# Decoder trunk on one core: the latent projection as one pass over x, and the last output block cut in two

## The chip, the cores and the metric

The kernel runs on one core of a Trainium2 chip. The metric is device time in microseconds of one launch: the median of three runs of the kernel before is 759.71 us (758.45 to 760.53). One further execution was recorded by the profiler; every duration below comes from that one.

## What is computed

A trunk of two pre-norm residual layers on x of 256 tokens by 2048 features, in float32. Layer a is multi-head latent attention, layer b is MoBA attention, which at 256 tokens is causal attention with ALiBi. Cut to what the change touches:

```python
h    = rms_norm(x, norm_a)
proj = h @ w_in_a                         # 2048 x (512 + 256 + 64 + 2048)
q_lat, kv_lat, k_rope, gate = split(proj, [512, 768, 832])
q    = rms_norm(q_lat,  q_lat_norm)  @ w_q_up
kv   = rms_norm(kv_lat, kv_lat_norm) @ w_kv_up
x    = x + (attention(q, kv, k_rope) * silu(gate)) @ w_out_a
x    = x + moba_layer(x)                  # ends with  ... @ w_out_b, 2048 x 2048
```

The first 832 columns of `w_in_a` are "the latents" (`LAT`). The row scale of the RMS norm of x is applied after the projection; the gain is folded into x before it.

## The kernel before

x lies transposed in SBUF as 16 chunks k of 128 features by 256 tokens (tile `xt`). A float32 product is made of three fp32r products: x and the weights are each split into a high part (`xh`, `wh`) and a low part (`xl`, `wl`), and xh·wh + xh·wl + xl·wh are summed in PSUM. ACT makes the high part and DVE the low part, of x in `split_x` (L313, L314), of a weight chunk in `W.high` and `W.low` (L146, L150). A weight chunk is at most 1024 columns of 128 partitions, fetched by one DMA on SP's queue (L132); there are 4 buffers for raw chunks, 4 for high parts, 3 for low parts, and `run` fetches 4 chunks ahead of the step that TensorE is at.

Two builders make the steps of a product, one step for each k. `blk_rows` lets the weights move through TensorE past a stationary piece of x: tokens come out on partitions, in two token halves, each in one PSUM bank (`acc`, five banks). `blk_cols` does the reverse. All matmuls have the helper's line L198 and are chained, so TensorE runs them in exactly the order of the program.

That order comes from two lists. `main` holds the projections in the order in which they are written; `side` holds what lies between them (norms, transposes, scores, softmax, products with v) with the time after which each is assumed ready. `ordered` walks both with assumed costs and puts a side step in as soon as it is ready by that clock. `flip` transposes through a DMA on SP's queue.

The start: the latents were made in two passes over x, `lat0` for columns 0 to 415 and `lat1` for columns 416 to 831, 16 steps of 6 matmuls of 416 columns each. `lat0` has chunks of one k, one k, and then two k (832 columns); x arrives in pieces of one or two chunks of 128 features, each loaded just ahead of the weight chunk that needs it and split just ahead of the step. The four sums of squares (`squares`) lie in `lat1`, then come `gates[0]` (16 steps) and `gates[1][:HALF]` (3 steps) before the first head group, `group_a(0)`. The side chain of the latents runs meanwhile: `col_a` (sums over partitions, tile `ps_st`; the row scale `r_a`), `row_a` (`ps_r`), `lat_out` (scales the latents out of PSUM into `sf`, then their own norm), `lat_t` (transposes, `ps_lt`, and the split into `xt`), and then `group_a(0)` may start.

The end: `outs_b` are four blocks of 512 output columns, two PSUM banks each. `out_done_b` adds each bank to x (L856) and stores it as 256 KB on SP's queue (L857).

Of the kernel before, what the change touches and what calls it, by code (L numbers as in the profile page):

```python
# [26 lines left out]
ALU = mybir.AluOpType  # L27

P = 128
S = 256  # L30
DM = 2048
NC = DM // P
# [1 line left out]
EPS = 1e-6  # L34
WARM = 34
ACC = 5
HALF = 3


NR, NH, NW = 4, 4, 3  # L40
# [6 lines left out]
PA, PB, LO, TU, TUB, S1, S2A, S2B, S3 = 9000, 6000, 5000, 3000, 10000, 4800, 6000, 9000, 3000  # L47
# [6 lines left out]
LAT = QR + KVR + ROPE  # L54
# [22 lines left out]
def paired(v):  # L77

    return v.rearrange("p (g l e) -> p g e l", l=2, e=16)


def lines(v):

    return v.rearrange("p (g l e) -> p g l e", l=2, e=16)


def unpaired(v):

    return v.rearrange("p (g e l) -> p g l e", l=2, e=16)
# [3 lines left out]
def trunk(ctx: ExitStack, tc, xT, gains, cst, w_in_a, w_q_up, w_kv_up, w_out_a, w_in_b, w_out_b, outT):  # L93
    nc = tc.nc
# [7 lines left out]
    def acc(name):  # L102
        return pacc.tile([P, 512], F32, tag="acc", name=name)
# [86 lines left out]
    def chain(ins):  # L190

        if pe:
            tc.add_manual_dep(ins.ins, pe[-1].name, mybir.DependencyInfo(
                mybir.DependencyClass.NoSync, mybir.DependencyReason.DATA), reason="order")
        pe.append(ins.ins)

    def matmul(*args, **kw):
        chain(nc.tensor.matmul(*args, skip_group_check=True, **kw))  # L198
# [4 lines left out]
    def blk_rows(w, x, done, lag=PB, first=()):  # L203

        nk, n = w.shape[0] // P, w.shape[1]
        a = []

        def go(wt, c, k):
            xh, xl = x()
            if k == 0:  # L210
                a.extend(acc("acc") for _ in range(2))
            for t in range(2):
                ts = slice(t * P, (t + 1) * P)
                o = a[t][:, :n]
                matmul(o, xh[:, k, ts], paired(wt.h[:, c]), start=k == 0, stop=False)
                matmul(o, xh[:, k, ts], paired(wt.l[:, c]), start=False, stop=False)
                matmul(o, xl[:, k, ts], paired(wt.h[:, c]), start=False, stop=k == nk - 1)
            if k == nk - 1:
                done([a[t][:, :n] for t in range(2)])

        return _steps(w, go, 6 * (n / 2.4 + 2.5), lag, first, True)

    def blk_cols(w, x, done, lag=3000):

        nk, ns = w.shape[0] // P, w.shape[1] // P
        a = []

        def go(wt, c, k):
            xh, xl = x()
            if k == 0:  # L230
                a.extend(acc("acc") for _ in range(ns // 2))
            for s in range(ns):
                o = a[s // 2][:, (s % 2) * S:(s % 2 + 1) * S]
                ws = slice(s * P, (s + 1) * P)
                first = k == 0 and s % 2 == 0
                last = k == nk - 1
                matmul(o, wt.h[:, c, ws], paired(xh[:, k]), start=first, stop=False)
                matmul(o, wt.h[:, c, ws], paired(xl[:, k]), start=False, stop=False)
                matmul(o, wt.l[:, c, ws], paired(xh[:, k]), start=False, stop=last)
            if k == nk - 1:  # L240
                done(a)

        return _steps(w, go, 3 * ns * 109, lag)

    def _steps(w, go, cost, lag, first=(), moving=False):
        out, nc_w = [], 1024 // w.shape[1]
        nk = w.shape[0] // P
        k1 = 0
        for n in list(first) + [nc_w] * nk:
            k0, k1 = k1, min(k1 + n, nk)  # L250
            if k0 == nk:
                break
            wt = W(w[k0 * P:k1 * P], moving)
            for k in range(k0, k1):
                out.append(Step(lambda wt=wt, c=k - k0, k=k: go(wt, c, k), cost, lag if k == nk - 1 else 0,
                                w=wt if k == k0 else None))
        return out
# [30 lines left out]
    xh = one.tile([P, NC, S], F32R, name="xh")  # L288
    xl = one.tile([P, NC, S], F32R, name="xl")
# [21 lines left out]
    def split_x(c, gcol):  # L311
        xt = res["x"]
        res["split"] = nc.scalar.activation(xh[:, c], xt[:, c], AF.Copy, scale=col(gcol + c))  # L313
        nc.vector.scalar_tensor_tensor(xl[:, c], xt[:, c], col(gcol + c), xh[:, c].bitcast(F32),  # L314
                                       op0=ALU.mult, op1=ALU.subtract)
# [45 lines left out]
    def gate_done(g, rows):  # L361
        def done(a):
            for b in range(len(a)):
                ub = wk.tile([P, 2, S], F32, tag="gate", name="gate", bufs=4)
                gate_of[g + b] = ub
                x = wk.tile([P, 2, S], F32, tag="gx", name="gx")
                nc.vector.tensor_tensor(x, a[b].rearrange("p (h t) -> p h t", h=2),
                                        rows().unsqueeze(1).to_broadcast([P, 2, S]), op=ALU.mult)
                nc.scalar.activation(ub, x, AF.Tanh, scale=0.5)
                nc.vector.scalar_tensor_tensor(ub, ub, 1.0, x, op0=ALU.add, op1=ALU.mult)  # L370
        return done
# [90 lines left out]
    main, side = [], []  # L462
# [14 lines left out]
    def x_load(c0, c1):  # L477
        return lambda: nc.sync.dma_start(res["x"][:, c0:c1], xT[c0 * P:c1 * P].rearrange("(c p) t -> p c t", p=P))

    def x_split(c0, c1):  # L480
        def f():
            for c in range(c0, c1):
                split_x(c, G_NA)
        return Step(f, 0, 1000)

    def rest():
        with tc.issue_after(lat1[0].w.dma):
            nc.sync.dma_start(g_sb[:, G_QN:G_END], gains[:, G_QN:])
            nc.sync.dma_start(c_sb, cst[:, :C_COS])

# [31 lines left out]
    lat_acc = []  # L522

    def lat_out(i):
        def f():
            o = i * LAT // 2
            for t in range(2):
                nc.scalar.activation(lat[t][:, o:o + LAT // 2], lat_acc[i][t], AF.Copy, scale=scale_a["r"][:, t:t + 1])
            if i:
                lat_norm()  # L530
        return f

    lat_st = {}

    def lat_norm():
        st = one.tile([P, 2, 3], F32, name="lat_st")
# [50 lines left out]

    x_a = lambda: (xh, xl)
    rows_a = lambda: scale_a["rows"]
    lat0 = blk_rows(w_in_a[:, 0:LAT // 2], x_a, lat_acc.append, 0, (1, 1))  # L590
    lat1 = blk_rows(w_in_a[:, LAT // 2:LAT], x_a, lat_acc.append, 0)
    gates = [blk_cols(w_in_a[:, LAT + 256 * g:LAT + 256 * (g + 1)], x_a, gate_done(g, rows_a)) for g in range(8)]

    def v_tiles():
# [94 lines left out]
        return proj  # L689

    pieces = [(0, 1), (1, 2), (2, 4), (4, 6), (6, 8), (8, 10), (10, 12), (12, 14), (14, 16)]
    for i, (c0, c1) in enumerate(pieces):
        main += [x_split(c0, c1)] + lat0[c0:c1]
        for j in ((1, 2) if i == 0 else (i + 2,)):
            if j < len(pieces):
                lat0[pieces[j][0]].w.before = x_load(*pieces[j])
    squares = [Step(lambda j=j: sum_squares(ssq_a, 2 * j) or sum_squares(ssq_a, 2 * j + 1), 0, 2500) for j in range(4)]
    main += lat1[:2] + [Step(rest)]
    for j in range(4):
        main += [squares[j]] + lat1[2 * j + 2:2 * j + 4]  # L700
    main += lat1[10:] + gates[0] + gates[1][:HALF]
    col_a, row_a = token_scale(ssq_a, "a", scale_a, squares, tables)
    lo = [Step(lat_out(i), 0, LO, [col_a], b[-1:]) for i, b in enumerate((lat0, lat1))]
    lo[1].after.append(lo[0])
    lats = [Step(lat_t(b), 440, 2500, lo, bank=True) for b in range(3)]
    kr = Step(kr_t, 440, 2500, lats, bank=True)
# [26 lines left out]
    og = lambda: (ogh, ogl)  # L733
    outs_a = [blk_cols(w_out_a[:, 256 * j:256 * (j + 1)], og, out_done_a(j), 4000) for j in range(8)]

    for g in range(8):
        main += group_a(g)
        if g == 0:
            kr.after.append(main[-1])
        if g < 7:  # L740
            main += gates[g + 1][HALF:] + (gates[g + 2][:HALF] if g < 6 else [])
        gates[g][-1].after.append(row_a)
        if g > 3:
            gates[g][-1].after += [h[2] for h in heads[2 * g - 8:2 * g - 6]]
# [101 lines left out]
        side.extend(s for h in hb[-4:] for s in h)  # L846
        return gate + q + k + v

    def out_done_b(j):
        def f(a):  # L850
            xt = res["x"]
            for b in range(2):
                c = 4 * j + 2 * b
                y = xt[:, c:c + 2]
                both = lines(y.rearrange("p a b -> p (a b)"))
                nc.vector.tensor_tensor(both, unpaired(a[b]), both, op=ALU.add)  # L856
                nc.sync.dma_start(outT[c * P:(c + 2) * P].rearrange("(c p) t -> p c t", p=P), y)  # L857
        return f

    outs_b = [blk_cols(w_out_b[:, 512 * j:512 * (j + 1)], og, out_done_b(j)) for j in range(4)]  # L860

    col_b, row_b = token_scale(ssq_b, "b", scale_b, [outs_a[7][-1]], scales_b)
    side += [col_b, row_b]
# [3 lines left out]
    for b in outs_b:  # L867
        for i, s in enumerate(b):
            s.needs.append(hb[i][2])
    main += outs_b[0][:12] + outs_b[1][:6] + outs_b[0][12:] + outs_b[1][6:] + outs_b[2] + outs_b[3]  # L870
    run(ordered(main, side))


# [59 lines left out]
```

## Time and profile before

| | |
|---|---|
| median of three runs | 759.71 us (758.45 to 760.53) |
| the profiled execution | 760.14 us |
| its span, first to last instruction | 758.0 us |
| TensorE (PE) busy in the span | 746.2 us |
| VectorE (DVE) busy | 576.2 us |
| ScalarE (ACT) busy | 488.3 us |
| mean granted TensorE clock | 0.998 of full speed |

The profiled execution took 760.14 us, of which the span of its instructions is 758.0 us; 2.14 us lie around it. PE is TensorE's matmuls, DVE is VectorE, ACT is ScalarE, SP the engine whose queue issues nearly all DMAs. A row of the timeline gives the start in us from the start of the span, the duration, the engine, the line, the operation with its output and inputs by the program's names, and in brackets how long the engine had been idle and what released it. Matmuls are pipelined, so that one shows a longer duration than its distance to the next.

### The profile page before, as it was taken

How to read it: one execution, taken by the hardware profiler on the slowest of the kernel's cores; microseconds unless marked ns; L12 is line 12 of the kernel's file. 1: busy time of each engine (PE TensorE's matmuls, PEld its weight loads, DVE VectorE, ACT ScalarE, POOL GpSimd, SP SyncE). 2: the span in 40 equal slices, each digit the busy share in tenths (PEclk: the TensorE clock that was granted, in tenths of full speed). 3: DMA queues.
4: the chain of work that ended last, by engine and by line, in shares of the span. 5: the costliest groups of instructions: out<-in, count | busy, mean ns of one | idle time of the engine just before them, and what ended most of it. 6: DMA issues, size and time to landing. Idle time of an engine off the chain costs nothing.

```text
span 758.0 us, 14123 instructions
## 1 busy us (share of the span) xinstructions
PE 746.2 (98%) x5246; PEld 708.0 (93%) x5246; DVE 576.2 (76%) x1207; ACT 488.3 (64%) x1025; POOL 0.2 (0%) x4
## 2 busy tenths in 40 slices
PE   8999999999999899999999999999999999999997
PEld 7999999999999899998889988998889988899997
DVE  6888899898997585765888767886688857887552
ACT  7767888888877464545667566665567666574431
POOL 0000000000000000000000000000000000000000
PEclk9999999999999999999999999999999999999999
DMA  9866665666557966667886778876788778867771
GB/s 304 257 177 180 185 177 167 181 156 185 162 167 222 248 195 199 196 189 202 228 234 174 200 221 229 229 188 208 188 240 230 188 211 220 231 181 215 250 223 44
DMA packets 137973, 153.19 MB, mean 202 GB/s; under 512 B 47280, under 2 KB 94768, under 8 KB 137904
## 3 DMA queue, kind: packets, MB, share of 16 engines
q1 hardware_dynamic: 137760, 152.27, 70.7%
q8 instruction: 41, 0.67, 0.4%
q14 instruction: 28, 0.23, 0.1%
q10 hardware_dynamic: 144, 0.02, 0.0%
HBM read 139.68 MB, written 2.10 MB: 187 GB/s over the span
## 4 chain that ended last, share of the span: by engine, by line
PE 66%; DMA 1%; ACT 0%; DVE 0%; issue 0%; SPq 0%
PE acc L198 63%; PE ps_o L198 1%; PE ps_s L198 1%; DMA sm<-pz 1%; ACT wh L146 0%; DVE xt L856 0%; DVE pz L409 0%; PE ps_r L198 0%; PE ps_st L198 0%; ACT alibi L819 0%; SPq L408 0%; DVE pl L440 0%; ACT pz L407 0%; ACT ogh L455 0%; ACT sm L426 0%
## 5 line engine op out<-in xcount | busy, mean ns | idle before, releaser
L146 ACT ACTIVATE wh<-wr 128x1024 fp32r<-128x1024 f32 (+3 forms) x265 | 288.0, 1091 | 161.3 <-PE acc L198 144.0
L150 DVE TENSOR_TENSOR wl<-wr,wh 128x1024 fp32r<-128x1024 f32 (+3 forms) x265 | 313.9, 1187 | 90.6 <-PE acc L198 59.1
L198 PE MATMUL acc<-wh,xh 128*128 128x512 f32 (+1 forms) x448 | 168.6, 376 | 1.4 <-ACT wh L146 1.4
L198 PE MATMUL acc<-wl,xh 128*128 128x512 f32 (+1 forms) x448 | 167.5, 374 | 1.0 <-DVE wl L150 1.0
L198 PE MATMUL acc<-wh,xl 128*128 128x512 f32 (+1 forms) x448 | 167.2, 373 | 0.0
L198 PE MATMUL acc<-ogh,wh 128*128 128x256 f32 x512 | 142.7, 279 | 0.0
L198 PE MATMUL acc<-xh,wh 128*128 128x256 f32 x512 | 142.4, 278 | 0.0
L198 PE MATMUL acc<-ogl,wh 128*128 128x256 f32 x512 | 141.7, 277 | 0.0
L198 PE MATMUL acc<-ogh,wl 128*128 128x256 f32 x512 | 141.6, 276 | 0.0
L198 PE MATMUL acc<-xh,wl 128*128 128x256 f32 x512 | 140.8, 275 | 0.0
L198 PE MATMUL acc<-xl,wh 128*128 128x256 f32 x512 | 140.8, 275 | 0.0
L198 PEld LDWEIGHTS acc<-ogh,wl 128*128 128x128 f32 x512 | 99.1, 194 | 0.0
L198 PEld LDWEIGHTS acc<-ogl,wh 128*128 128x128 f32 x512 | 99.0, 193 | 0.1
L198 PEld LDWEIGHTS acc<-ogh,wh 128*128 128x128 f32 x512 | 99.0, 193 | 0.0
L198 PEld LDWEIGHTS acc<-xl,wh 128*128 128x128 f32 x512 | 98.2, 192 | 0.3
L198 PEld LDWEIGHTS acc<-xh,wh 128*128 128x128 f32 x512 | 98.2, 192 | 0.3
L198 PEld LDWEIGHTS acc<-xh,wl 128*128 128x128 f32 x512 | 98.3, 192 | 0.0
L198 PEld LDWEIGHTS acc<-wh,xh 128*128 128x128 f32 x448 | 84.7, 189 | 12.1 <-ACT wh L146 2.0
L198 PEld LDWEIGHTS acc<-wl,xh 128*128 128x128 f32 x448 | 84.7, 189 | 11.7 <-DVE wl L150 1.7
L198 PEld LDWEIGHTS acc<-wh,xl 128*128 128x128 f32 x448 | 84.7, 189 | 10.3
L198 PE MATMUL acc<-wh,xt 128*128 128x384 f32 (+1 forms) x192 | 57.5, 357 | 0.0
L409 DVE COPY pz<-sm 128x768 uint16<-128x768 uint16 x32 | 19.4, 605 | 22.7 <-DMA sm<-pz 22.4
(154 smaller groups left out, 841.1 us busy)
## 6 DMA issues: line engine op xcount, KB each, us to landing
wr<-w_in_b SPq DMA_DIRECT2D x128, 512.0 KB, 4.3
wr<-w_in_a SPq DMA_DIRECT2D x32, 512.0 KB, 4.0
wr<-w_out_a SPq DMA_DIRECT2D x32, 512.0 KB, 4.0
wr<-w_out_b SPq DMA_DIRECT2D x32, 512.0 KB, 4.6
wr<-w_in_a SPq DMA_DIRECT2D x15, 416.0 KB, 5.3
wr<-w_q_up SPq DMA_DIRECT2D x16, 384.0 KB, 3.8
wr<-w_kv_up SPq DMA_DIRECT2D x8, 512.0 KB, 3.8
xt<-xT SPq DMA_DIRECT2D x4, 512.0 KB, 5.7
```

The costliest lines, as they stand in the source:

```text
L146: nc.scalar.activation(self.ordering(self.h)[1], self.ordering(self.raw)[0], AF.Copy)
L150: nc.vector.tensor_tensor(self.ordering(self.l)[1], self.ordering(self.raw)[0], self.ordering(self.h.bitcast(F32))[1], op=ALU.subtract)
L198: chain(nc.tensor.matmul(*args, skip_group_check=True, **kw))
L409: nc.vector.tensor_copy(words(b), planes(a))
```

## The change

It does four things.

1. `blk_latents` replaces `lat0` and `lat1`: one pass over x, each k with both halves of the latents. The first k has two chunks of 416 columns, the other 15 have one chunk of 832 columns. The four accumulators (two halves, two token halves) are open at once. In a step the order is xh·wh, xl·wh, xh·wl, each for both token halves, first for the first half of the columns and then for the second.
2. x's pieces and the sums of squares follow that pass: a piece of two chunks is split, then come two steps of 12 matmuls; each `squares` step lies behind the piece that completes its four chunks. The load of the constants (`rest`) moves behind k = 5.
3. `HALVES` replaces `HALF`: 8 steps of `gates[1]` instead of 3 lie ahead of `group_a(0)`, then 6, 4 and from there on 3 as before.
4. The last 512 output columns become two blocks of 256 columns (one bank each); the very last is added in two halves of 128 rows by 256 tokens and stored in two pieces, one issued by SP and one by ACT.

```diff
-HALF = 3
+HALVES = [0, 8, 6, 4, 3, 3, 3, 3]
...
+    def blk_latents():
+        hf = LAT // 2
+        def go(wt, k, js):
+            if not lat_acc:
+                lat_acc.extend([acc("acc")[:, :hf] for _ in range(2)] for _ in range(2))
+            for i, j in enumerate(js):
+                ws = slice(i * hf, (i + 1) * hf)
+                wh, wl = paired(wt.h[:, 0, ws]), paired(wt.l[:, 0, ws])
+                for x, w, first, last in ((xh, wh, True, False), (xl, wh, False, False), (xh, wl, False, True)):
+                    for t in range(2):
+                        matmul(lat_acc[j][t], x[:, k, t * P:(t + 1) * P], w,
+                               start=k == 0 and first, stop=k == NC - 1 and last)
+        def step(k, js):
+            wt = W(w_in_a[k * P:(k + 1) * P, js[0] * hf:(js[-1] + 1) * hf], True)
+            return Step(lambda: go(wt, k, js), 6 * len(js) * 176, 0, w=wt)
+        return [step(0, (0,)), step(0, (1,))] + [step(k, (0, 1)) for k in range(1, NC)]
...
-    lat0 = blk_rows(w_in_a[:, 0:LAT // 2], x_a, lat_acc.append, 0, (1, 1))
-    lat1 = blk_rows(w_in_a[:, LAT // 2:LAT], x_a, lat_acc.append, 0)
+    latent = blk_latents()
...
-    for i, (c0, c1) in enumerate(pieces):
-        main += [x_split(c0, c1)] + lat0[c0:c1]
-        for j in ((1, 2) if i == 0 else (i + 2,)):
-            if j < len(pieces):
-                lat0[pieces[j][0]].w.before = x_load(*pieces[j])
-    main += lat1[:2] + [Step(rest)]
-    for j in range(4):
-        main += [squares[j]] + lat1[2 * j + 2:2 * j + 4]
-    main += lat1[10:] + gates[0] + gates[1][:HALF]
+    main += [x_split(0, 1)] + latent[:2]
+    for i, (c0, c1) in enumerate(pieces[1:]):
+        latent[c0 + 1].w.before = x_load(c0, c1)
+        main += [x_split(c0, c1)] + [squares[j] for j in range(4) if c1 == (6, 10, 14, 16)[j]] + latent[c0 + 1:c1 + 1]
+        if c1 == 6:
+            main += [Step(rest)]
+    main += gates[0] + gates[1][:HALVES[1]]
...
-    lo = [Step(lat_out(i), 0, LO, [col_a], b[-1:]) for i, b in enumerate((lat0, lat1))]
+    lo = [Step(lat_out(i), 0, LO, [col_a], latent[-1:]) for i in range(2)]
...
-            main += gates[g + 1][HALF:] + (gates[g + 2][:HALF] if g < 6 else [])
+            main += gates[g + 1][HALVES[g + 1]:] + (gates[g + 2][:HALVES[g + 2]] if g < 6 else [])
...
-    def out_done_b(j):
+    def out_done_b(c0, m, queues):
         def f(a):
             xt = res["x"]
-            for b in range(2):
-                c = 4 * j + 2 * b
-                y = xt[:, c:c + 2]
+            for i in range(2 * len(a) // m):
+                c, o = c0 + m * i, m * i * S
+                y = xt[:, c:c + m]
                 both = lines(y.rearrange("p a b -> p (a b)"))
-                nc.vector.tensor_tensor(both, unpaired(a[b]), both, op=ALU.add)
-                nc.sync.dma_start(outT[c * P:(c + 2) * P].rearrange("(c p) t -> p c t", p=P), y)
+                nc.vector.tensor_tensor(both, unpaired(a[o // 512][:, o % 512:o % 512 + m * S]), both, op=ALU.add)
+                queues[i % len(queues)].dma_start(outT[c * P:(c + m) * P].rearrange("(c p) t -> p c t", p=P), y)
         return f
-    outs_b = [blk_cols(w_out_b[:, 512 * j:512 * (j + 1)], og, out_done_b(j)) for j in range(4)]
+    out_b = lambda c0, c1, *how: blk_cols(w_out_b[:, c0 * P:c1 * P], og, out_done_b(c0, *how))
+    outs_b = [out_b(4 * j, 4 * j + 4, 2, (nc.sync,)) for j in range(3)]
+    outs_b += [out_b(12, 14, 2, (nc.sync,)), out_b(14, 16, 1, (nc.sync, nc.scalar))]
```

What this does to the order of the instructions, at the three places that matter. First SP's queue at the very start, before the change: x's pieces (`xt`) and the chunks of 416 or two times 416 columns (`wr`) alternate.

```order
L468 DMA xt_72<-xT 128x256
L132 DMA wr_131<-w_in_a 128x416
L478 DMA xt_72<-xT 128x256
L132 DMA wr_133<-w_in_a 128x416
L478 DMA xt_72<-xT 128x2x256
L132 DMA wr_136<-w_in_a 128x2x416
```

The same queue after the change:

```order
L468 DMA xt_72<-xT 128x256
L132 DMA wr_131<-w_in_a 128x416
L132 DMA wr_133<-w_in_a 128x416
L478 DMA xt_72<-xT 128x256
L132 DMA wr_135<-w_in_a 128x832
L478 DMA xt_72<-xT 128x2x256
L132 DMA wr_138<-w_in_a 128x832
```

Ahead of the second x chunk there is now the other half of the first k's weights, and a weight chunk of 832 columns holds one k instead of two.

Second ACT between the latents and their norm, before the change (`wh` of 1024 columns belongs to the gates, `sf` is the latents scaled out of PSUM, `sq` the squares for their norm):

```order
L146 ACTIVATE wh<-wr 128x1024 x3
L528 ACTIVATE sf_124<-acc,r_a 128x416
L528 ACTIVATE sf_125<-acc,r_a 128x416
L146 ACTIVATE wh<-wr 128x1024
L528 ACTIVATE sf_124<-acc,r_a 128x416
L528 ACTIVATE sf_125<-acc,r_a 128x416
L542 ACTIVATE sq,lat_st<-sf_124 128x512
```

After the change:

```order
L146 ACTIVATE wh<-wr 128x1024 x5
L528 ACTIVATE sf_124<-acc,r_a 128x416
L528 ACTIVATE sf_125<-acc,r_a 128x416
L528 ACTIVATE sf_124<-acc,r_a 128x416
L528 ACTIVATE sf_125<-acc,r_a 128x416
L146 ACTIVATE wh<-wr 128x1024
L564 ACTIVATE sq,lat_st<-sf_124 128x512
```

Two more weight chunks stand ahead of the first scaling, and none between the four scalings.

Third SP's queue at the end, before the change:

```order
L857 DMA outT<-xt 128x2x256 x2
L132 DMA wr<-w_out_b 128x2x512 x8
L857 DMA outT<-xt 128x2x256 x2
L132 DMA wr<-w_out_b 128x2x512 x2
L857 DMA outT<-xt 128x2x256 x2
```

After the change:

```order
L877 DMA outT<-xt 128x2x256 x2
L132 DMA wr<-w_out_b 128x4x256 x2
L877 DMA outT<-xt 128x2x256
L877 DMA outT<-xt 128x256
```

The store of the first of the two new blocks stands ahead of the last 128 KB that SP issues; the other 128 KB are ACT's last instruction.

From the seventh head group of layer a to the last 512 output columns, the order of all engines is the same as before.

## Rows read from the trace of the kernel before

**Rows 1.** the page: busy time by engine, and the granted clock in 40 slices

```profile
PE 746.2 (98%) x5246; PEld 708.0 (93%) x5246; DVE 576.2 (76%) x1207; ACT 488.3 (64%) x1025; POOL 0.2 (0%) x4
...
PEclk9999999999999999999999999999999999999999
```

**Rows 2.** waits of PE: who for, us in total, times, longest us

```profile
PE ps_o L198 <- ACT ph L439: 2.7, 1, 2.7
PE acc L198 <- DVE wl L150: 1.9, 8, 0.6
PE acc L198 <- ACT wh L146: 1.4, 2, 0.8
```

**Rows 3.** timeline of PE, 4 to 43 us: start, us, work, [idle before <-releaser]

```profile
4.53 0.42 PE L198 MATMUL acc<-wh,xh 128*128 128x416 f32 x1
...
6.83 0.44 PE L198 MATMUL acc<-wh,xh 128*128 128x416 f32 x1 [0.57 <-ACT wh L146]
...
9.40 0.44 PE L198 MATMUL acc<-wh,xh 128*128 128x416 f32 x1 [0.79 <-ACT wh L146]
10.46 0.44 PE L198 MATMUL acc<-wl,xh 128*128 128x416 f32 x1 [0.62 <-DVE wl L150]
...
11.09 0.34 PE L198 MATMUL acc<-wl,xh 128*128 128x416 f32 x1
...
37.81 0.61 PE L198 MATMUL ps_st<-ones,ssq 128*128 128x128 f32 x4
38.18 0.42 PE L198 MATMUL acc<-wh,xh 128*128 128x416 f32 x1
...
42.48 0.27 PE L198 MATMUL acc<-xh,wh 128*128 128x256 f32 x1
```

**Rows 4.** timeline of ACT, 6 to 13 us: waits for weight chunks

```profile
6.20 0.58 ACT L146 ACTIVATE wh<-wr 128x416 fp32r<-128x416 f32 x1 [1.17 <-DMA wr<-w_in_a]
...
8.39 0.95 ACT L146 ACTIVATE wh<-wr 128x832 fp32r<-128x832 f32 x1 [0.61 <-DMA wr<-w_in_a]
...
12.20 1.00 ACT L146 ACTIVATE wh<-wr 128x832 fp32r<-128x832 f32 x1 [0.20 <-DMA wr<-w_in_a]
```

**Rows 5.** timeline of all engines, 39 to 54 us

```profile
39.05 0.15 DVE L341 TENSOR_SCALAR rv_a<-ps_st 128x2 f32<-128x2 f32 x1
...
52.59 1.41 DVE L552 TENSOR_SCALAR sf<-sf,rs_y 128x512 f32<-128x512 f32 x4
...
53.19 0.30 PE L201 MATMUL ps_lt<-c_sb,sf 128*128 128x128 f32 x1
53.80 0.55 PE L201 MATMUL ps_lt<-c_sb,sf 128*128 128x128 f32 x3 [0.31 <-DVE sf L552]
```

**Rows 6.** timeline of PE and DVE, 97 to 101 us: a group's last turn

```profile
97.87 0.38 PE L201 MATMUL ps_ta<-c_sb,ra 128*128 128x128 f32 x2
...
100.69 0.28 DVE L392 SCALAR_TENSOR_TENSOR sr<-ps_ta,sr 128x128 fp32r<-128x128 f32 x1
```

**Rows 7.** timeline of PE, 251 to 257 us: the long wait and after

```profile
251.88 0.38 PE L198 MATMUL ps_o<-ph,vh 128*128 128x256 f32 x1 [2.67 <-ACT ph L439]
...
254.04 0.42 PE L198 MATMUL acc<-ogl,wh 128*128 128x256 f32 x1
...
256.39 0.42 PE L198 MATMUL acc<-ogh,wh 128*128 128x256 f32 x1
```

**Rows 8.** timeline of all engines, 753 us to the end

```profile
753.32 1.36 DVE L856 TENSOR_TENSOR xt<-acc,xt 128x512 f32<-128x512 f32 x2 [6.09 <-PE acc L198]
...
753.67 0.28 PE L198 MATMUL acc<-ogh,wl 128*128 128x256 f32 x1
754.03 1.05 SPq L857 DMA_DIRECT2D outT<-xt  x2
```

**Rows 9.** DMA view, 745 to 758 us: GB/s in 40 slices; issues to landing

```profile
GB/s 0 0 0 0 0 0 0 0 50 0 0 0 0 0 0 0 0 0 0 0 0 0 0 0 0 0 0 0 0 0 120 343 344 344 353 110 0 0 0 0
...
outT<-xt SPq DMA_DIRECT2D x2, 256.0 KB, 2.2
```

More of the change, by code (lines that the diff above doesn't have):

```diff
@@ L486, in rest @@
     def rest():
-        with tc.issue_after(lat1[0].w.dma):
+        with tc.issue_after(latent[7].w.dma):
             nc.sync.dma_start(g_sb[:, G_QN:G_END], gains[:, G_QN:])
@@ L869, in trunk @@
             s.needs.append(hb[i][2])
-    main += outs_b[0][:12] + outs_b[1][:6] + outs_b[0][12:] + outs_b[1][6:] + outs_b[2] + outs_b[3]
+    main += outs_b[0][:12] + outs_b[1][:6] + outs_b[0][12:] + outs_b[1][6:] + sum(outs_b[2:], [])
     run(ordered(main, side))
```

## The prediction

> **What bounds the kernel now.** I read the page first. TensorE is busy for 746.2 us of a span of 758.0 us, and its clock is granted nearly all the time [rows 1]. The change takes no matmul away (the count is the same), so it can only win back idle time of PE or shorten what lies behind the last matmul. The question is where that idle time lies. The waits of PE show three large items [rows 2]: one of 2.7 us for `ph`, and together 3.3 us for the low and high parts of weight chunks (1.9 and 1.4). The timeline puts all of the latter into the first 10.5 us [rows 3]: 0.57 us ahead of k = 1, 0.79 ahead of k = 2, and 0.62 for the low part that follows. ACT, which makes the high parts, shows what is behind this: it sat idle until a weight chunk had landed, at 6.20, 8.39 and 12.20 us [rows 4]. So the start is bound by the loads of x and weights and the rest by TensorE; the wait of 2.67 us at 251.88 [rows 7] lies where all engines' order stays the same, and I leave it in. Behind the last matmul (753.67 us) come two additions and two stores of 256 KB [rows 8].
>
> My sum is against the profiled execution, 760.14 us; the median of 759.71 us is 0.43 us lower, and I take that off at the end.
>
> **The start: one pass instead of two.** The matmuls of the latents come every 0.1758 us: 152 steps from 11.09 to 37.81 us [rows 3]. All 192 need 33.75 us. They run from 4.53 to 42.48 us, less 0.37 us for the sums `ps_st` in between (37.81 to 38.18) [rows 3]: 37.58 us. So 3.83 us are lost now.
>
> The new pass needs less per matmul: for one k it loads 128 KB of x and 416 KB of weights for 12 matmuls, where the first old pass loaded 128 and 208 KB for 6. When the chunks land I take from what ACT waited for [rows 4]. Counting bytes in the order of SP's queue, 672 KB had landed at 6.20 us, 1344 KB at 8.39 and 2688 KB at 12.20. In the new order the chunk of k = 1 is complete at 128 + 208 + 208 + 128 + 416 = 1088 KB, between the first two: 6.20 + 416/672 x 2.19 = 7.56 us. The chunk of k = 2 is complete at 1760 KB: 8.39 + 416/1344 x 3.81 = 9.57 us. From a chunk of 832 columns having landed to its first matmul took 1.01 us (8.39 to 9.40), to the first one with its low part 2.07 us (8.39 to 10.46) [rows 3, 4]. So k = 1 starts at about 8.57 us. In the new step four matmuls come ahead of the low part, which is there at 7.56 + 2.07 = 9.63 us; eight matmuls remain, and k = 1 ends at 11.04 us. The low part of k = 2 is ready at 9.57 + 2.07 = 11.64 us, and PE wants it at 11.04 + 4 x 0.176 = 11.74 us: no wait. From there one k takes 2.11 us on PE; the chunks need 544 KB in that time, below the 1344 KB in 3.81 us that rows 4 show. ACT and DVE have the same splits and squares to do as in both old passes together. So the other 14 k end at 11.04 + 14 x 2.11 = 40.58 us, with `ps_st` 40.95, against 42.48 us: **1.53 us gained**.
>
> The bounds: the chunk of k = 1 can't land before the 672 KB at 6.20 us nor after the 1344 KB at 8.39. At 8.39 the low part is there at 10.46, k = 1 ends at 11.87, and the gain is 0.70 us. At 6.20, with k = 2's chunk at 8.39 at best, k = 2 ends at 11.87 and the gain is 1.53 + 13.15 - 11.87 = 2.81 us (13.15 is k = 2's end in my sum). I keep the interpolated value, because 1088 KB lies well inside a measured stretch.
>
> **The latents' norm: less cover, another mix in front.** `ps_st` was 24 latent matmuls ahead of the pass's end; now it stands behind it. PE needed 53.19 - 37.81 = 15.38 us from it to the first transpose `ps_lt` [rows 3, 5]. Now 24 latent matmuls (4.22 us) leave that stretch and 36 more gate matmuls enter; at 256/416 of 0.1758 us these are 3.9 us. The cover shrinks by 0.3 us. The chain under it (DVE's row scale from 39.05 us, ACT's scaling and squares, DVE's norm, the scaling of `sf` at 52.59) released PE at 53.80, already too late by a recorded 0.31 us [rows 5]. What queues in this chain changes both ways: two more weight chunks ahead of ACT's first scaling and a gate's multiplication inside DVE's norm, but no chunk between the four scalings and none inside the row scale. I take the chain as long as before and charge the lost cover, **0.3 us**; from below, -0.3 (the chain gets shorter by as much as the recorded wait), from above 1.2 us (one low part more in it: 2.07 - 1.01 = 1.06 us, rounded up). Behind `ps_lt` one step less lies ahead of `group_a(0)`, but its first matmuls need only the first of six chunks, so nothing is charged.
>
> **The groups.** The 8, 6 and 4 gate steps move work ahead of group 0 and leave fewer steps later. The tightest place that I find is group 1: between its last turn `ps_ta` and the scores there are now 6 matmuls of 384, 6 of 512 columns and one `ps_o`, by columns 2.3 + 0.4 us plus the transposes, about 2.9 us. The turn's last low part was ready 3.1 us after the turn began (97.87 to 100.69 + 0.28) [rows 6]. The scores need it only in their second half. I charge **0.1 us** (0 to 0.5). Other distances stay above 4 us.
>
> **The end.** The first of the two new blocks is stored long before the end. For the last, both halves lie in one bank, and in the changed order only the first addition waits for PE: it therefore waits for the block's last matmul, until about 753.95 us (753.67 + 0.28) [rows 8]. Before, one addition of 0.68 us already ran by then and the second ended at 754.68. Two halves of about 0.4 us, overlapping a little, end at about 754.75: the last store is issued 0.07 us later than before. But it is 128 KB, and 256 KB instead of 512 KB move in all. At the 344 GB/s that the stores reached [rows 9] the last piece takes 0.38 instead of 0.76 us. Gain **0.3 us**; at worst -0.07 (a store's 2.2 us [rows 9] don't depend on its size), at best 0.31. I take the upper value, as the rate stands in a row.
>
> In the Trainium skill, "DMA: Bandwidth & Descriptors" (section "Anatomy of one DMA") makes a DMA a fixed 2 us plus bytes at 436 GB/s. By that estimate half of 256 KB saves 0.3 us and the end 0.23 us; rows 9 give 0.31. The same page ("Issuing engines are not separate DMA queues") says that a second issuing engine saves only the time to issue, so by it ACT's queue adds nothing here; no run shows that yet.
>
> **The sum.** 1.53 - 0.3 - 0.1 + 0.3 = 1.43 us. 760.14 - 1.43 = 758.71; less 0.43, **758.3 us**.
>
> **The rivals.**
> - *Loads keep up.* The start gains its bound of 2.81 us, nothing is charged later: 2.81 + 0.3 = 3.1, so 756.6 us. For it: larger chunks, fewer issues by SP per byte. Against: rows 4 show the slowest progress exactly between 6.20 and 8.39 us.
> - *The clock falls at the start.* PE now stands still once, from the end of k = 0 (12 matmuls from 4.53 us and a short wait for its second chunk: about 6.9 us) to 8.57, about 1.7 us. After waits of 0.79 and 0.62 us the clock stayed up [rows 1, 3]; after 2.67 us the matmuls of 256 columns came every 0.214 us (11 steps from 254.04 to 256.39) [rows 7], which is the lower level, 1.2 GHz. Eleven such steps instead of 0.108 us cost 1.2 us: 759.5 us. Late landing (k = 1 at 8.39 us) ends at the same place: 758.3 + 0.8 = 759.1.
> - *The norm's chain slips.* If the gate's multiplication and two weight chunks each add their length, about 2.4 us, the wait at `ps_lt` reaches that of rows 7, and the clock falls with it: 2.4 + 1.2 in place of the 0.3 charged, 758.3 + 3.3 = 761.6 us, **slower than before**. It decides once the chain is over 1.6 us longer than its cover was; for it speaks that the wait exists already, against it that two items also leave the chain.
> - *The end doesn't do what it says.* No gain there: 758.6 us; inside my forecast's own range.
>
> "TensorE: Matmul & The Clock Gate" of the Trainium skill (section "What's actually happening") says that the clock is granted by how busy TensorE has been lately. Rows 7 agree with it, and rows 3 bound it from the other side; by that rule alone the second rival would be the forecast, 759.5 us.
>
> **How the numbers follow.** Forecast 0.58 (757.4 to 759.2 us), loads keep up 0.20, clock or late landing 0.14, norm's chain 0.08. A difference under 0.3%, 2.3 us, can hardly be told from none here. Faster by more (below 757.4): the first rival and the lower edge of the forecast, 0.25. Slower by more (above 762.0): the upper part of the last rival, 0.05. Within: 0.70. The range from 756.5 to 760.3 us leaves out the last rival and the far edge of the first.
>
> **What would show it.** In the profile after: one wait of some 1.7 us ahead of k = 1, none at k = 2, the latents' end near 41 us with `ps_st`; PE's sum of waits for weight parts down from 3.3 to about 2 us; a wait at `ps_lt` of 0.3 to 0.9 us; the 2.67 us at `ps_o` unchanged; the last issue of a store at 1.1 us behind the start of the last matmul, and the span's end 0.3 us closer to it. It is wrong if matmuls in the first 15 us take twice as long, if PE waits for a weight part after k = 2, or if a new wait over 1 us stands between 45 and 170 us.

## The result and the profile after

The changed kernel takes 766.67 us (median of 6 runs, 764.01 to 768.91) where the kernel before took 759.08 in the same comparison: 1.0104 times as long, with a 95% interval from 1.0087 to 1.0121. It is slower by 1.0%, 7.6 us. Where one launch took far longer than all the others (1101 us in pass_covered below, 1924 us of the kernel before), the ratio leaves it out and the median does not. The profiled execution spans 764.1 us, where it was 758.0.

The page's line on the engines, to set beside [rows 1], shows TensorE busy for 1.0 us more, with the same count of matmuls, and idle for 16.9 us of the span, where it was 11.8:

```profile
PE 747.2 (98%) x5246; PEld 709.2 (93%) x5246; DVE 575.6 (75%) x1208; ACT 485.4 (64%) x1025; POOL 0.2 (0%) x4
```

The view by windows says where. Columns: the stretch, its length, the busy time of PE with its matmuls, the granted clock, the DMA engines' busy share, GB/s. First the kernel before:

```profile
0.00:50.00 50.00, 46.49 (x295) 1.00 0.87 269
50.00:100.00 50.00, 49.69 (x391) 1.00 0.60 167
100.00:150.00 50.00, 49.49 (x377) 1.00 0.64 175
150.00:200.00 50.00, 49.60 (x394) 1.00 0.63 169
```

and the changed kernel:

```profile
0.00:50.00 50.00, 48.45 (x309) 1.00 0.85 269
50.00:100.00 50.00, 46.72 (x356) 0.97 0.55 152
100.00:150.00 50.00, 47.27 (x367) 1.00 0.61 158
150.00:200.00 50.00, 46.84 (x359) 1.00 0.63 173
```

Subtract each busy time from 50. The first 50 us have 1.96 us less idle time: the new pass gains there, as was forecast. From 50 to 200 us the idle time rises from 1.22 to 9.17 us. Some 0.9 us of that is the wait of the latents' norm, before 60 us; the other 7 us lie in the stretch of the head groups, where I had charged 0.1 us.

The waits of PE (who for, us in total, times, longest us), to set beside [rows 2], name new releasers:

```profile
PE ps_o L198 <- ACT ph L439: 2.2, 2, 1.8
PE ps_s L198 <- DVE sr L392: 2.2, 3, 1.5
PE acc L198 <- DVE rs_t L307: 2.1, 1, 2.1
PE ps_o L198 <- DVE sr L392: 1.4, 1, 1.4
PE acc L198 <- DVE wl L150: 1.3, 1, 1.3
PE acc L198 <- DVE tok L660: 1.2, 1, 1.2
```

Two of them are of a kind that [rows 2] don't have at all: an `acc` matmul waits for `rs_t` or `tok`, which it doesn't read. Its inputs are there; what it lacks is a place to write.

**The wait at 75 us.** The timeline of PE and DVE, 67 to 77 us (start, us, work, [idle before <-releaser]):

```profile
66.92 0.60 PE L201 MATMUL ps_kr<-c_sb,krz 128*128 128x128 f32 x4
67.28 0.36 PE L198 MATMUL acc<-xh,wh 128*128 128x256 f32 x1
...
72.61 0.28 PE L198 MATMUL acc<-xh,wl 128*128 128x256 f32 x1
...
74.96 0.55 PE L198 MATMUL acc<-xh,wh 128*128 128x256 f32 x1 [2.08 <-DVE rs_t L307]
75.31 0.42 PE L198 MATMUL acc<-xl,wh 128*128 128x256 f32 x1
```

```profile
72.41 0.17 DVE L303 TENSOR_SCALAR rs_y<-ga_v 128x12 int32<-128x12 int32 x1
...
74.13 0.68 DVE L367 TENSOR_TENSOR gx<-acc,rr_a 128x512 f32<-128x512 f32 x1
...
76.36 0.28 DVE L657 TENSOR_TENSOR rp<-acc,rs_y 128x128 f32<-128x128 f32 x1
76.56 0.41 DVE L660 TENSOR_TENSOR tok<-acc,rs_y 128x256 f32<-128x256 f32 x1
```

There are five accumulators (`ACC = 5`). Group 0 has filled four by 66.9 us, and they are emptied on DVE by `rp` and `tok`, which scale the group's projections out of PSUM, from 76.36 us on. Gate 1 holds the fifth; its last eight steps run from 67.28 to 72.72 us. Gate 2 comes next and finds none free. The first one to come free is gate 1's own, by DVE's `gx`, and `gx` stands in DVE's order inside the inverse square roots of group 0 (L303 to L308); it runs from 74.13 to 74.81 us. PE starts again 0.15 us behind it, 7.7 us after the group's end; `rs_t`, which the row names, is only what DVE did next. In the kernel before 13 steps (8.7 us) of gate 1 lay behind group 0, so gate 2 came later than that and found a place. Behind the wait, matmuls of 256 columns come every 0.21 us instead of 0.11: the lower level of the clock, 1.2 GHz, until about 78.4 us. The 16 matmuls up to there take 3.48 us, 1.7 us more than at 0.11 us each.

"Perfetto Trace Analysis" of the Trainium skill (section "Matmuls") asks that independent groups of matmuls rotate through PSUM banks, so that emptying one overlaps filling the next. The trace agrees: here the rotation ran out for 2.08 us.

**The wait at 108.5 us** is of another kind. It is 1.50 us at the scores of group 1, for the low part of the keys (`sr`). DVE's timeline shows what held that up:

```profile
104.75 1.22 DVE L150 TENSOR_TENSOR wl<-wr,wh 128x1024 fp32r<-128x1024 f32 x1
107.24 0.60 DVE L409 COPY pz<-sm 128x768 uint16<-128x768 uint16 x1 [1.27 <-DMA sm<-pz]
107.73 0.74 DVE L392 SCALAR_TENSOR_TENSOR sr<-ps_ta,g_sb,sr 128x512 fp32r<-128x512 f32 x1
```

DVE works in its own order. It stood still for 1.27 us for the transposing DMA of an earlier head, and the low part of the keys was queued behind. At 122.27 us follows another wait for an accumulator (1.24, `tok`), and at 197.95 and 200.27 two of 1.38 (`sr`) and 1.26 (a low part of a weight chunk). These two stand behind the same kind of stop:

```profile
195.85 0.60 DVE L409 COPY pz<-sm 128x768 uint16<-128x768 uint16 x1 [1.96 <-DMA sm<-pz]
```

A smaller form of these two comes without the new numbers: end_only (below), with the old ones, has a stop of DVE of 1.69 us at the same place and waits of PE of 0.20 and 1.26 us behind it.

**The start, the norm and the end** stayed close to the forecast or inside its bounds, but for 0.09 us at the end. ACT's wait for the chunk of k = 1, beside [rows 4], and then rows of PE, beside [rows 3, 5]:

```profile
7.29 0.98 ACT L146 ACTIVATE wh<-wr 128x832 fp32r<-128x832 f32 x1 [1.46 <-DMA wr<-w_in_a]
```

```profile
8.33 0.62 PE L198 MATMUL acc<-wh,xh 128*128 128x416 f32 x2 [0.28 <-ACT wh L146]
...
40.44 0.61 PE L198 MATMUL ps_st<-ones,ssq 128*128 128x128 f32 x4
...
56.55 0.30 PE L201 MATMUL ps_lt<-c_sb,sf 128*128 128x128 f32 x1 [0.89 <-issue]
57.16 0.55 PE L201 MATMUL ps_lt<-c_sb,sf 128*128 128x128 f32 x3 [0.31 <-DVE sf L574]
```

The end, beside [rows 8]: from the start of the last matmul to the end of the span 3.93 us, where it was 4.33 (758.0 - 753.67).

```profile
760.17 0.28 PE L198 MATMUL acc<-ogh,wl 128*128 128x256 f32 x1
760.48 0.76 DVE L876 TENSOR_TENSOR xt<-acc,xt 128x256 f32<-128x256 f32 x2 [6.76 <-PE acc L198]
...
761.27 0.35 ACTq L877 DMA_DIRECT2D outT<-xt  x1
```

### The profile page after: what moved, and what is told of

The parts are those of the page before. It is cut to its first block, busy times and chain, and to the rows that moved or that the text cites. A ratio compares the mean times of both kernels' runs of the same rounds, so it can differ in the third digit from the quotient of the medians.

```text
span 764.1 us, 14120 instructions
## 1 busy us (share of the span) xinstructions
PE 747.2 (98%) x5246; PEld 709.2 (93%) x5246; DVE 575.6 (75%) x1208; ACT 485.4 (64%) x1025; POOL 0.2 (0%) x4
## 4 chain that ended last, share of the span: by engine, by line
PE 65%; DMA 1%; ACT 0%; issue 0%; DVE 0%; DVEq 0%
PE acc L198 63%; PE ps_o L198 1%; PE ps_s L198 1%; DMA sm<-pz 1%; ACT wh L146 0%; DVE pz L409 0%; PE ps_r L198 0%; PE ps_st L198 0%; DVE xt L876 0%; DVEq L951 0%; ACT pz L407 0%; DVE pl L440 0%; ACT alibi L838 0%; ACT ogh L455 0%; ACT sm L426 0%
## 5 line engine op out<-in xcount | busy, mean ns | idle before, releaser
L198 PE MATMUL acc<-wh,xh 128*128 128x512 f32 (+1 forms) x448 | 163.6, 377 | 0.3 <-ACT wh L146 0.3
L198 PE MATMUL acc<-wl,xh 128*128 128x512 f32 (+1 forms) x448 | 162.3, 374 | 0.1
L198 PE MATMUL acc<-wh,xl 128*128 128x512 f32 (+1 forms) x448 | 162.4, 374 | 0.0
```

## The experiments

Theory A: the numbers in `HALVES` cause the loss, because they take gate steps from between the first groups. Theory B: the pass itself upsets what follows. Ratios are against the kernel before, with 95% intervals.

**pass_half3: the pass and the end, with the old numbers.**

```diff
-HALVES = [0, 8, 6, 4, 3, 3, 3, 3]
+HALVES = [0, 3, 3, 3, 3, 3, 3, 3]
```

> The changed kernel with the old number of gate steps ahead of each group again (3 everywhere, so 16 steps between one group and the next); the one pass over x and the new end stay. Theory A (the new numbers 8, 6, 4 took the gate steps from between the first groups, and with them the cover for the chains on VectorE and ScalarE and for the accumulator banks): the waits for rs_t at 75 us (2.08), for sr at 108.5 (1.50) and for tok at 122 (1.24) go; the wait ahead of ps_lt grows from 1.2 us by up to five steps of 0.67 us, 3.3 us, and the clock may fall with it (about 1.8 us). Sum: 766.7 - 4.8 + 3.3, so 763 to 767 us, with all new time at ps_lt and nothing between 65 and 190 us. Theory B (the pass itself, by its place of the row scale behind the latents' end, upsets everything behind it): the waits of over 1 us between 65 and 200 us stay, 767 us or more.

Measured: 758.95 us, ratio 1.0003 (0.9987 to 1.0020). Theory A holds: nothing of over 0.25 us is left between 60 and 230 us. But the time is below my range: I had expected the wait ahead of the transposes to grow by 3.3 us. The waits there add up to 1.7 us, 0.5 us more than in the changed kernel; the first `ps_lt` stands at 54.64 us instead of 56.55. The chain under them is not of fixed length: from `ps_st` to the end of the last wait at `ps_lt` it takes 14.54 us here (40.80 to 55.34) and 16.72 in the changed kernel, where five more gate steps lie ahead. PE's timeline there:

```profile
55.34 1.39 PE L201 MATMUL ps_lt<-c_sb,sf 128*128 128x128 f32 x11 [0.40 <-DVE sf L574]
57.61 0.43 PE L198 MATMUL acc<-wh,xt 128*128 128x384 f32 x1 [0.88 <-ACT xt L596]
58.65 0.59 PE L198 MATMUL acc<-wh,xt 128*128 128x384 f32 x2 [0.45 <-DVE xt L597]
```

**halves_only: the kernel before with the new numbers alone.**

```diff
-HALF = 3
+HALVES = [0, 8, 6, 4, 3, 3, 3, 3]
```

> The kernel before with nothing changed but the numbers of gate steps ahead of the groups, 0, 8, 6, 4, 3, 3, 3, 3 in place of 3 everywhere. Theory A: the loss comes from them alone; the waits at about 77, 110 and 124 us come (together some 4.8 us, and about 1.8 us of the lower clock), the wait of 0.31 us at ps_lt goes: 763 to 766 us. Theory B: no new wait over 1 us, the time within 1 us of before, 758 to 760 us.

Measured: 768.03 us, ratio 1.0119 (1.0089 to 1.0150), more than theory A's range and far from B's. Its waits of PE are those of the changed kernel, with the old pass over x:

```profile
PE acc L198 <- DVE rs_t L307: 2.4, 1, 2.4
PE ps_s L198 <- DVE sr L392: 2.2, 3, 1.5
...
PE acc L198 <- DVE tok L639: 1.2, 1, 1.2
```

So this one table makes the whole loss: 8.9 us alone, and none is left without it (pass_half3).

**gates8 and gates14: what about the table costs.** Both are the changed kernel with other numbers. gates8 keeps 16 steps between the groups, but each gate ends 8 steps behind the group. gates14 has 14 steps between groups 0 and 1, but gate 1 ends 13 steps behind group 0.

```diff
-HALVES = [0, 8, 6, 4, 3, 3, 3, 3]
+HALVES = [0, 8, 8, 8, 8, 8, 8, 8]     (gates8)
+HALVES = [0, 3, 1, 0, 0, 0, 0, 0]     (gates14)
```

> The changed kernel with 0, 8, 8, 8, 8, 8, 8, 8 gate steps ahead of the groups: 16 steps stand again between any two groups (8 of the one gate, 8 of the next), but each gate still ends 8 steps, 5.3 us, after the group ahead of it, where in the kernel before it ended 13 steps, 8.7 us, after. Theory A1 (accumulator banks: a group holds four of the five, and the next gate can only start when a bank has been emptied, some 7.5 us after the group's end): a wait of 1.2 to 2.5 us at the first step of the next gate, put down to rs_t or tok, stays at 75 us and comes at nearly every later group, some 10 us of them; 770 us or more. Theory A2 (only the number of steps between groups counts): no wait for rs_t or tok; waits that are left stand at the end of the groups, where 8 steps now lie ahead of the last one; 762 to 766 us.

Measured: 768.67 us, ratio 1.0114 (1.0089 to 1.0139). The wait at gate 2 stays, though 16 steps lie between the groups (PE's timeline):

```profile
73.97 0.35 PE L198 MATMUL acc<-xh,wh 128*128 128x256 f32 x1 [2.07 <-DVE rs_t L307]
...
95.81 0.35 PE L198 MATMUL acc<-xh,wh 128*128 128x256 f32 x1 [0.98 <-DVE tok L660]
```

So at this gate it is the accumulators (A1), not the number of steps. But the waits for `rs_t` and `tok` add up to 3.6 us (2.07, 0.98 and 0.51), not to the 10 that A1 priced, and the time lies between the ranges of the two theories. Larger waits stand at the last groups, where A2 had put them (0.99 us at 197 us and 2.78 at `ps_o`, at 220 us).

> The changed kernel with 0, 3, 1, 0, 0, 0, 0, 0 gate steps ahead of the groups: 14 steps between groups 0 and 1 as in the changed kernel, 15 between 1 and 2, then 16; but gate 1 ends 13 steps after group 0. Theory A1 (banks): no wait for rs_t or tok anywhere; the wait for sr of 1.5 us ahead of group 1's scores may stay, as it is one of cover. Theory A2 (number of steps): waits of over 1 us stay both behind group 0 and ahead of the scores of group 1. Time by A1 759 to 761 us, by A2 762 us or more.

Measured: 763.58 us, ratio 1.0048 (1.0033 to 1.0064). No wait for `rs_t` or `tok` is left, which is A1 again. But the time is above A1's range: low parts come late (PE's timeline):

```profile
75.62 0.43 PE L198 MATMUL acc<-wl,xt 128*128 128x384 f32 x1 [1.11 <-DVE wl L150]
...
147.00 0.51 PE L198 MATMUL ps_s<-sr 128*128 128x256 f32 x2 [1.32 <-DVE sr L392]
```

Only the first of these stands behind one of the short distances (14 steps, ahead of group 1). The one at 147 us lies in group 4, and one of 1.06 us at 206.97 us behind group 6; ahead of those groups 16 steps lie as in the kernel before, but none of the next gate's steps stands ahead of a group. So this run does not show that the number of steps costs. From pass_half3 (ratio 1.0003) to gates14 (1.0048) the table costs some 0.45% with no wait for an accumulator in the trace, and from there to the changed kernel (1.0104) some 0.55% more, where such waits are. The runs do not separate the two further, since each table also moves work at the later groups. No run changed the number of accumulators: that they are what was short at 75 and 122 us is read from the traces and from these two tables.

**end_only: the kernel before with the new end.** The diff is the last part of the change (`out_done_b`, `outs_b`).

> The kernel before with the new end alone (last 512 columns as two blocks, the last stored in two pieces). Both theories: from the start of the last matmul to the end of the span 3.9 us, where it was 4.3, so 0.4 us less, 758.7 us. If the end gives nothing: 4.3 us and 759.1.

Measured: 759.75 us, ratio 1.0005 (0.9988 to 1.0021). Timing can't see it; the trace can: from the start of the last matmul to the end of the span it is 3.91 us (754.49 to 758.4). In all nine profiles with the new end it lies between 3.9 and 4.0 us, in the three with the old end it is 4.33.

**early_x and pass_covered: giving the norm its cover back.** Both have the pass, the end and 3 steps everywhere, and load, split and square part of x ahead of its use, so that `ps_st` comes well ahead of the latents' end. pass_covered loads fewer blocks ahead and raises the time that the planner assumes for the norm.

```diff
+    ahead = [0, 0, 0, 1, 2, 3, 4, 5]     (early_x)
+    ahead = [0, 0, 0, 0, 0, 1, 2, 3]     (pass_covered)
...
-        latent[c0 + 1].w.before = x_load(c0, c1)
+        k = c0 - ahead[i]
+        latent[k + 1].w.before = x_load(c0, c1)     (x_split and squares move to k with it)
...
-PA, PB, LO, ... = 9000, 6000, 5000, ...
+PA, PB, LO, ... = 9000, 6000, 6500, ...  (pass_covered)
```

> The new pass and end, 3 gate steps everywhere, and x loaded, split and squared up to 5 row blocks ahead of its use in the pass (the loads of x from row block 6 on move ahead by 1, 2, 3, 4 and 5), so that the row scale is summed again well ahead of the latents' end. Theory A: the pass keeps its 1.7 us, the end its 0.4, the chain at ps_lt its cover (no wait over 0.5 us there), and no new wait over 1 us stands before 190 us: 759.1 - 2.1, so 756.5 to 758 us. Theory B: as the pass still shifts everything behind it, waits of over 1 us stand between 65 and 200 us, 762 us or more. If loads of x that come earlier hold up the weights: waits for weight parts of over 1 us before 30 us, about 759 us.

Measured: 760.43 us, ratio 1.0001 (0.9980 to 1.0022). Missed. PE waited 0.74 us for a low part at 27.50 us, where pass_half3, which differs in the earlier loads, splits and squares of x alone, has no wait. The 1.43 us ahead of k = 1 are not theirs, since the chunks up to there are loaded as in pass_half3 (1.06 us) and gates8 (1.72). And PE waited 1.80 and 0.40 us at `ps_lt`, although gate steps were left: the planner had set the transposes at the end of an assumed 6.5 us (`LO` x 1.3), and the chain took 8.9 us (from the start of the latents' last matmul at 43.1 us to 51.95).

> The kernel of the run best with the reload of x put back to where it was before. What it is to tell: what the new pass and the new end are worth together where the norm behind the latents has its cover. By the profile of best (no wait at ps_lt, 1.2 us at the start of the pass): the last matmul starts 749.8 + 1.1 (the late high part of a head goes) + 1.3 to 2.7 us of wait for ph, and 1.7 us more where the clock falls behind it; the end is 4.0 us; so 757 to 759 us. If the pass were worth nothing even with cover, 759.5 us or more.

Measured: 756.59 us, ratio 0.9955 (0.9935 to 0.9975), 0.4 us below the expected range. No wait at `ps_lt` is left, and behind it none of over 0.4 us up to the wait for `ph` at 250 us (1.54). So with cover for the norm and the old table the pass and the end together win about 3.4 us by the ratio (1.9 to 4.9). One profile would not have told it: the profiled executions of pass_covered and of pass_half3 took 757.83 us both; in that of pass_covered the clock fell behind the wait for `ph` (granted 0.50 from 252 to 254 us).

**late_reload, end_reload and best: the old wait of [rows 7].** The reload of x (2 MB) stood ahead of the last two heads' transposing DMAs on SP's queue; now it is planned behind their softmax. late_reload is the kernel before with that alone, end_reload adds the new end, best is pass_covered with it.

```diff
-    again = Step(reload, 0, 8000, (), [h[0] for h in heads[14:]] + main[-1:])
+    again = Step(reload, 0, 8000, (), [h[1] for h in heads[14:]] + main[-1:])
```

> The kernel before with one step moved: the reload of x (2 MB) and of a table is issued behind the softmax of the last two heads rather than ahead of it, so that their two transposing DMAs don't queue behind it on SP's queue. If that queue is the cause of the wait of 2.67 us for ph and of the half clock behind it: the transposes land in some 2.2 us rather than 6.3, the wait goes, and with it about 1.7 us of the lower clock: 755 to 757.5 us. If it is ScalarE or VectorE that hold ph back: 2 to 2.7 us of wait stay, 759 us.

Measured: 758.48 us, ratio 0.9985 (0.9967 to 1.0002). The time is above the expected range, but the cause is right. In the DMA view, 236 to 258 us (KB each, median us to landing), first before, then late_reload:

```profile
sm<-pz SPq DMA_TRANSPOSE x2, 6.3
```

```profile
sm<-pz SPq DMA_TRANSPOSE x2, 3.6
```

The transposes land in 3.6 us, not in the 2.2 expected. The wait for `ph` is gone from the trace, 0.42 us for `ogh` comes in its place, and the clock stays at its upper level there. But what that is worth was not told apart from nothing.

> The kernel before with the new end and the late reload, and the old two passes over x with everything at their heads as before. It differs from best in the pass, in the early loads of x and in the assumed time of the norm alone. By the profiles: late_reload's 758.5 less 0.4 for the end, 758 us; if the pass is worth nothing, 755.8 us, as best.

Measured: 757.65 us, ratio 0.9973 (0.9954 to 0.9992), near the 758 us expected from the traces.

> The new pass and end, 3 gate steps everywhere, x from row block 10 on loaded ahead by 1, 2 and 3, the planner's assumed time of the latents' norm raised from 5000 to 6500 ns (it was 8.9 us measured, times 1.3 is 8.45), and the reload of x behind the last two heads' softmax. Sum of what the runs showed: pass 1.7, end 0.4, no wait at ps_lt 0.3, no wait for ph 2.7 and its clock 1.7: 759.1 - 6.8, so 752.5 to 755 us. Against: the three parts were each worth nothing that could be measured (pass_half3 759.0, early_x 760.4); if the start stays like that, only the reload's part is left, 755 to 757 us.

Measured: 755.77 us, ratio 0.9953 (0.9936 to 0.9970): 3.6 us faster than the kernel before by the ratio (4.2 by the medians). That is short of the 752.5 to 755 us hoped for, inside the 755 to 757 of the other case, and not told apart from pass_covered. Its largest waits of PE behind the warm-up:

```profile
PE acc L198 <- DVE wl L150: 1.5, 6, 0.4
...
PE acc L198 <- ACT wh L146: 1.2, 1, 1.2
PE acc L198 <- ACT ogh L455: 1.1, 1, 1.1
```

What the pass alone is worth (best against end_reload) and what the reload is worth (best against pass_covered) lies inside the intervals and stays open.

## Why the prediction was wrong, step by step

- **The start: right.** Forecast 1.53 us with `ps_st` done at 40.95; measured 40.44 + 0.37 = 40.81 against 42.48, 1.67 us. The chunk of k = 1 was there at 7.29 us (forecast 7.56) and k = 1 started at 8.33 (forecast 8.57); in the seven profiles with the new pass it starts between 8.05 and 8.71. Only the wait ahead of it, 0.28 us and not 1.7, came out otherwise, because k = 0 ended at 8.05 us and not at 6.9: its first six matmuls came every 0.28 to 0.42 us and not every 0.176, with no wait shown between them. In gates8, with the same order up to here, k = 0 ran at full pace and the forecast wait is there:

```profile
8.54 0.62 PE L198 MATMUL acc<-wh,xh 128*128 128x416 f32 x2 [1.72 <-ACT wh L146]
```

  The clock did not fall behind that wait either (granted 1.00 from 8 to 20 us). So neither rival at this place (all loads keep up, the clock falls) came.
- **The norm: inside its bounds, but not for the reason charged.** I charged 0.3 us of lost cover and took the chain as long as before. Measured are 1.20 us of wait at `ps_lt` against 0.31, so 0.9 us, inside the bound of 1.2. From `ps_st` to the end of the last wait the chain took 16.72 us (40.44 to 57.16) against 15.99 (37.81 to 53.80), 0.73 us more, while PE's work over it shrank only from 15.38 to 15.22 us. DVE began the row scale 2.79 us behind the start of `ps_st`, where it had been 1.24 [rows 3, 5]: a low part of a weight chunk stood ahead of it, the item of my upper bound.

```profile
42.08 1.23 DVE L150 TENSOR_TENSOR wl<-wr,wh 128x1024 fp32r<-128x1024 f32 x1 [1.39 <-ACT wh L146]
43.23 0.15 DVE L341 TENSOR_SCALAR rv_a<-ps_st 128x2 f32<-128x2 f32 x1
```

  The rival in which this chain makes the kernel slower did not come: the loss lies elsewhere.
- **The groups: the step that failed.** "Other distances stay above 4 us", with 0.1 us charged and 0.5 as the bound. PE's order gives what was lost there. Group 0 starts at 60.43 us (57.73 in the kernel before), with five more gate steps of 0.67 us ahead of it, so 0.65 us earlier than its work would have it; group 7 starts 9.0 us later, with the same work ahead of it (before, then after):

```profile
205.37 0.33 PE L198 MATMUL acc<-wh,xt 128*128 128x384 f32 x1
```

```profile
214.37 0.33 PE L198 MATMUL acc<-wh,xt 128*128 128x384 f32 x1
```

  The groups lose 9.65 us, then. The two waits for accumulators (2.08 and 1.24) and the lower clock behind the first (1.7) are 5.0 of it; the three waits behind a transposing DMA in DVE's order (1.50, 1.38, 1.26) are 4.1, of which end_only has 1.5 without the new numbers. Two things were wrong. I measured only the way from a group's turns (its transposes, `ps_ta`) to its scores, by columns on PE, and took the table for a plain move of work. And I treated a gate's step as ready whenever its weights are, and never counted accumulators: with four of five held by a group and the fifth by the gate that ends behind it, the gate after that could start only 7.7 us behind the group. The planner doesn't count them either. I also took the duration of the turns' low parts from one row [rows 6] and not their place in DVE's order, where a transposing DMA can stand ahead of them.
- **The wait for `ph`: expected unchanged, and shorter by luck.** It was 1.80 us at 260.18 us instead of 2.67, and the clock did not fall behind it (granted 1.00 from 260 to 265 us). From group 7 to the last matmul this gives back 2.5 us, which hides that much of the loss: 9.65 - 0.65 - 2.5 - 0.4 is the 6.1 us between the two spans. Its length differs from run to run: 1.27 in pass_half3, 1.64 in end_only. That it hangs on how the transposes fall among the reload's packets is likely after late_reload, but not shown.
- **The end: right in mechanism, a little larger.** Forecast 0.30, bounds -0.07 to 0.31; measured 0.40, and why it goes beyond the bound is open. The last store is issued 1.10 us behind the start of the last matmul, as I had said. For DMAs that GpSimd issues, the Trainium skill's "DMA: Bandwidth & Descriptors" (section "Anatomy of one DMA") gives a fixed cost of about 2 us plus the bytes at 436 GB/s; by that estimate the end would have gained 0.23 us. These stores are issued by SP and ACT, and the pieces of 128 KB landed 1.7 and 1.8 us after issue, so the trace has less than that fixed cost alone.
- **The rivals as a whole.** I had one case for slower, at 0.08, and put it at the norm. The table of eight numbers was the part of the change with most places to go wrong, and got the least of the argument. My last paragraph named the sign that came: new waits over 1 us between 45 and 170 us.

## What to carry to other kernels

When work is moved to cover one wait, look at what it covered where it was: each gate step taken from between two groups also gave VectorE time to empty accumulators. Count the accumulators for each stretch, held and free, and ask of every step not only whether its inputs are there but which instruction, on which engine and behind what else in that engine's order, frees the place that it writes to. An assumed chain time in a planner is worth checking against the trace: raising one constant toward what was measured, together with earlier loads of x, turned the same pass from no gain (pass_half3) into 0.45% (pass_covered). Which of the two did it was not tested; more early loads without the constant gained nothing (early_x).

## What was not expected of the hardware

- The clock after a wait of PE is no fixed function of the wait's length. After 2.08 us at 75 us it fell to 1.2 GHz in the changed kernel; after 2.07 us at the same place in gates8 the profile shows 1.00 throughout. It fell after 1.54 us in pass_covered and not after 1.80 us in the changed kernel. Much of the spread between launches goes with it: of the 29 launches of the kernel before beside gates8, the 13 with a mean granted clock of 1.0 took 757.51 to 760.49 us, the seven with 0.995 took 761.54 to 762.45. Windows of gates8 and of the changed kernel:

```profile
73.00:78.00 5.00, 4.03 (x36) 1.00 0.75 212
```

```profile
75.00:76.00 1.00, 1.00 (x5) 0.50 1.03 365
```

- The old start is less steady than one profile showed. In two of the five profiles with the old pass (end_only, late_reload) the granted clock from 10 to 20 us was 0.83, and `ps_st` came at 39.7 us, in the other three at 37.33 to 37.81; in none of the seven with the new pass did it fall.
